# GpSimd's additions of gate weights placed behind a head's diagonal blocks and its substitution, and given out four copies late instead of two

## The chip, the cores and the metric

The kernel runs on one core of a Trainium2 chip. The metric is device microseconds of one execution. Times are medians of several runs; the profile is one further execution.

## The reference

One residual block: a gated delta rule and a Conformer convolution run side by side on `x` (512 tokens of 1024 channels), are merged by sigmoid gates, and are followed by a SwiGLU layer and a last RMSNorm.

```python
h = rmsnorm(x, norm1_w)
q, k, v, z, b_raw, a_raw, glu, gates = split(h @ w_in)           # 1024 -> 8208
q, k, v = silu(causal_depthwise_conv(q|k|v, dn_conv_w))          # 8 heads of 128
# per head, chunks of 64 tokens:
t_mat = I + strict_lower(beta * (k k^T) * decay)                 # 64 x 64, unit lower triangular
u, w  = triangular_solve(t_mat, [v * beta, k * beta * exp(gc)])
v_new = u - w S ;  o = (q exp(gc)) S + (q k^T * decay) v_new ;  S = S * el + k_dec^T v_new
out_a = (rmsnorm(o) * silu(z)) @ dn_w_o
out_b = silu(layernorm(conv31(ga * sigmoid(gb)))) @ cm_w_pw2 + cm_b_pw2
x = x + (gate_a * out_a + gate_b * out_b) @ w_out
f_gate, f_up = split(rmsnorm(x) @ ffn_w_gate_up)                 # 1024 -> 2 * 2816
x = x + (silu(f_gate) * f_up) @ ffn_w_down
return rmsnorm(x, norm_f_w)
```

## The kernel before

**Products.** Nearly all matrix products are `split3` (L124): operand and weight are each split into a high and a low part, and three matmuls are added in PSUM. `unit` (L108 to L115) prepares one weight block: SP loads `raw` (L108), ScalarE (ACT) makes the high part `whi` (L113), VectorE (DVE) the low part `wlo` (L115). Each has three buffers.

**Stages.** The first part (to about 430 us in the profile) is the head phase: for each of 8 heads, here numbered 0 to 7, come the projections, a 4-tap convolution, `front` (the triangular matrix `Un`), the substitution, and later `chain` (inverse and recurrence). Between them stand the projections of the convolution branch and of the gates. Then come `dn_w_o`, `cm_w_pw2`, `w_out`, the second norm, the SwiGLU layer in Strassen-like form, and the end.

**One head on GpSimd (POOL).** In `front`: the root `nk` (L474), `Un` times the decay (L485, 128x512), four copies of the diagonal 32x32 blocks into `cp` (L492), and `cc` put together from them (L493 to L495). SP stores `cc` to DRAM and loads it back spread out as `U` (L497, L500). Then POOL inverts the 16x16 diagonal blocks in `y` by 15 steps of a multiplication and an addition (L508, L510): this is the substitution, and `last[0]` is its latest instruction. L448 adds the mask to the decays of two later heads. L666 takes the root for the output norm of a head that has ended.

**One head's chain.** `chain` joins the 16x16 inverses to 32x32, 64x64 and 128x128 blocks: ACT scales `y` into `YY` (L563, L564), DVE transposes it (L565) and adds (L568: `m`, 128x32, both inputs in SBUF), and TensorE (PE) multiplies (L532, in `group`, six products in pairs). The results go through ACT (`Q`, L577 and L593) and copies (L573, L585, L589). Then come four steps of the recurrence (L630, L631, L636, L644, L645 on PE; `w` L638 and `R` L641 on ACT; `o` L656 on DVE). Head h's chain runs while head h+1's `front` is under way.

**The gate weights' sums.** The SwiGLU layer needs sums of quarters of its weight, `s1` to `s4`, 19 of each. Each of the 76 is made ahead of time in DRAM: SP copies one quarter (L196, 256 KB), and when that has landed GpSimd adds another to it by a DMA that accumulates (L200). `feed_one` gives both out, one per prepared unit: the copy goes at the end of the list `begun`, and L200 is given out for the copy that is two behind. An L200 waits on POOL until its copy has landed, and POOL executes in order. SP also loads halves of the down-projection weight (L170), which POOL adds (L176) and stores (L177).

**What sets the order.** A scheduler places each engine's instructions by priorities and its own estimate of times; `issue_after` makes an instruction stand behind another one. On the chip each engine takes its list in order.

Of the kernel before, what the change touches and what calls it, by code (L numbers as in the profile page):

```python
# [10 lines left out]
ALU = mybir.AluOpType  # L11
# [13 lines left out]
START = 78  # L25
ROUND = 40
WARM = 9
OTHERS = (12, 12, 12, 12, 8, 8, 8, 8)
EPS = 1e-6

# [2 lines left out]
def block_kernel(ctx, tc, a):  # L33
    nc = tc.nc
    V, S, G, PE = nc.vector, nc.scalar, nc.gpsimd, nc.tensor
# [28 lines left out]
    half = small.tile([P, 1], F32, name="half")  # L64
# [31 lines left out]

    loads, start_feed, ahead, gps_ = [], [False], [False], []

    last = [None]

    def unit(ap, pool=None, after=None):

# [23 lines left out]
    def col_tile(ps, ap, xh, xl):  # L126
        hi, lo = unit(ap)
        for k in range(KD):
# [25 lines left out]
          for n, r, c in (("A11", 0, 0), ("A12", 0, 1), ("A21", 1, 0), ("A22", 1, 1))}  # L154


    feed = [("s1", 0), ("s1", 1)] + [(n, p + d + i) for p in range(0, FF - F0, 2)
                                     for n, d in (("s3", 0), ("s2", 0), ("s1", 2), ("s4", 0)) for i in range(2)]
    feed = [(*w, *{"s1": ("A21", gu["A22"]), "s3": ("A11", gu["A21"]), "s2": ("A11", sums["s1"]),
                   "s4": ("A12", sums["s2"])}[w[0]]) for w in feed if w[1] < FF - F0]  # L160
    fed, begun = [], []
# [28 lines left out]
    def feed_one(n=1):  # L190

        for _ in range(n):
            if feed:
                w, p, m, other = feed.pop(0)
                with tc.issue_after(loads[-1].ins):
                    nc.sync.dma_start(sums[w][p], gu[m][p])  # L196
                begun.append((sums[w][p], other[p]))
        while len(begun) > (2 if feed else 0):
            with tc.issue_after(fed[-1].ins) if fed else nullcontext():
                fed.append(nc.gpsimd.dma_start(*begun.pop(0), accum_op=ALU.add, max_dma_last_dim=2048))  # L200

    units, norming = [0], [False]
# [13 lines left out]
    with tc.tile_pool(name="st", bufs=2) as st:  # L216
# [43 lines left out]
        wps = psg.tile([P, T], F32, name="g")  # L260
        for i in range(WARM):
            PE.matmul(wps, warm.broadcast_to([P, P]), warm.broadcast_to([P, T]), start=True, stop=True)
# [10 lines left out]
        for k in range(KD):  # L273
# [3 lines left out]
                                   op0=ALU.mult, op1=ALU.subtract)  # L277
# [7 lines left out]
        ss = st.tile([P, 2, NT], F32, name="rms_ss", bufs=1)  # L285
# [60 lines left out]
        for k in range(2, 4):  # L346
# [6 lines left out]
                        in1=ss[:, 1].rearrange("p (n a) -> p n a", a=1).broadcast_to([P, NT, 16]), op=ALU.mult)  # L353
# [6 lines left out]
                        in1=rowp[:, 1:2, :].broadcast_to([P, NT, H]), op=ALU.add)  # L360
# [9 lines left out]
        with tc.issue_after(ln_.ins):  # L370
            for g_ in gated:
# [8 lines left out]
                        op=ALU.mult)  # L380
# [13 lines left out]
    def even_odd(t):  # L394
        return t.rearrange("p (q e) c -> p e q c", e=2)
# [40 lines left out]
    def tok(src, pool, tag):  # L436
        ps = pool.tile([P, 4, P], F32, name=tag)
        for n in range(NT):
            PE.transpose(ps[:, n, :], src[:, n, :], ident)  # L439
        return ps  # L440
# [20 lines left out]
    def front(h, kT, DT):  # L461
        sq = junk[:, 0:P]

        ss = gp.tile([P, 8, NT], F32, name="ss", bufs=5)
        ps = tok(kT, psg, "g")
        for n in range(NT):
            S.activation(sq, ps[:, n, :], AF.Square, accum_out=ss[:, 0, n:n + 1])
        kd = gp.tile([P, 3, P], F32, name="kd", bufs=3)
        for n in range(3):
            S.activation(kd[:, n, :], ps[:, n, :], AF.Copy, scale=kdf[:, n, h:h + 1])  # L470
        kk, rk, nk, nb2, b2 = ss[:, 3], ss[:, 4], ss[:, 5], ss[:, 6], ss[:, 7]
        V.tensor_scalar(out=kk, in0=ss[:, 0], scalar1=EPS, scalar2=None, op0=ALU.add)
        V.reciprocal(out=rk, in_=kk)
        G.tensor_tensor(out=nk, in0=kk, in1=root4, op=ALU.pow)  # L474
        V.tensor_tensor(out=nb2, in0=rk, in1=nbeta[:, :, h], op=ALU.mult)
        V.tensor_tensor(out=b2, in0=rk, in1=beta[:, :, h], op=ALU.mult)

        ps = psg.tile([P, 4, P], F32, name="g")
        for n in range(NT):
            PE.matmul(ps[:, n, :], kT[:, n, :], kT[:, n, :], start=True, stop=True)  # L480
        Un = gp.tile([P, NT, P], F32, name="Un", bufs=3)
        for n in range(NT):
            S.activation(Un[:, n, :], ps[:, n, :], AF.Copy, scale=nb2[:, n:n + 1])
        yield
        G.tensor_tensor(out=Un, in0=Un, in1=DT, op=ALU.mult)  # L485

        cp = gp.tile([P, NT, 32], F32, name="cp", bufs=3)
        cc = gp.tile([P, NT, 16], F32, name="cc")
        ct = gp.tile([P, NT, 16], F32, name="ct")
        for b in range(4):  # L490
            b32 = slice(32 * b, 32 * b + 32)
            G.tensor_copy(out=cp[b32].rearrange("p (e q) c -> p e q c", e=2), in_=even_odd(Un)[b32, :, :, b32])  # L492
        G.tensor_scalar(out=cc, in0=cp[:, :, 0:16], scalar1=mh1, scalar2=None, op0=ALU.mult)  # L493
        G.tensor_scalar(out=ct, in0=cp[:, :, 16:32], scalar1=mh2, scalar2=None, op0=ALU.mult)
        G.tensor_tensor(out=cc, in0=cc, in1=ct, op=ALU.add)  # L495
        sc = dram.tile([8, 16, NT, 16], F32, name="sc")
        nc.sync.dma_start(sc.rearrange("b k n c -> (b k) n c"), cc)  # L497
        U = gp.tile([P, 16, NT, 16], F32, name="U", bufs=2)
        for b in range(8):
            nc.sync.dma_start(U[16 * b:16 * b + 16].rearrange("p k n c -> p (k n c)"),  # L500
                              sc[b].rearrange("k n c -> (k n c)").partition_broadcast(16))

        y = gp.tile([P, NT, 16], F32, name="y", bufs=3)
        S.copy(out=y, in_=idc.rearrange("p (a c) -> p a c", a=1).broadcast_to([P, NT, 16]))
        for k in range(15):
            w = 15 - k
            tm = gp.tile([P, NT, 16], F32, name="ytm")
            G.tensor_tensor(out=tm[:, :, 0:w], in0=U[:, k, :, k + 1:],  # L508
                            in1=y[:, :, k:k + 1].broadcast_to([P, NT, w]), op=ALU.mult)
            last[0] = G.tensor_tensor(out=y[:, :, k + 1:], in0=y[:, :, k + 1:], in1=tm[:, :, 0:w], op=ALU.add)  # L510
        return ss, kd, b2, Un, cp, y
# [300 lines left out]
    def head(h, done):  # L812

        pk, pq = (yield from proj2()) if h == 0 else (None, None)
        k_ = yield from conv4(8 + h, "kT", pk)
        close()
        q_ = yield from conv4(h, "qT", pq)
        close()
        v = conv4(16 + h, "vT")
        for _ in range(2):  # L820
            next(v)
            yield
        DT = dts.pop(0)
        opening = front(h, k_, DT)
        if h == 0:
            with behind():
                next(opening)
            v_ = yield from v
        if raised:
            decay()  # L830
        if h % 2 == 0 and h + 2 < H:
            masked(h + 2, h + 3)
        with behind(), tc.issue_after(last[0].ins) if h else nullcontext():
            if h:
                next(opening)
            try:
                next(opening)
            except StopIteration as made:
                ss, kd, b2, Un, cp, y = made.value
        if h:  # L840
            v_ = yield from v
        pz = yield from proj(24 + h)
        z_ = zall[:, h, :]
        S.activation(z_, pz, AF.Silu)


        def second():
            Vp, at = front2(k_, q_, v_, DT, ss)
            done.append((h, k_, q_, ss, kd, b2, Un, cp, Vp, at, y, z_))
            yield 0  # L850

        chains.append([count[0] + 5, second()])
        yield
# [6 lines left out]
    def take(n):  # L860
        for _ in range(n):
            if next(rest, 0) == 0:
                return
            yield
# [4 lines left out]
    for h in range(H):  # L869
        queue.append(head(h, done))  # L870
        queue.append(take(OTHERS[h]))
    queue.append(rest)
    nh = 0
    while step() or chains:
        ahead[0] = count[0] >= 72
        start_feed[0] = count[0] >= 335
        if nh < H and count[0] >= START - 9 + 32 * nh + sum(OTHERS[:nh]):
            chains.append([0, chain(*done[nh])])
            nh += 1
        for c in list(chains):  # L880
            if c[0] <= count[0] or not queue:
                with behind():
                    n = next(c[1], None)
# [103 lines left out]
    def rms_half(ss, hf, n, cs, sq, last, y1=y1):  # L987

        S.activation(sq, y1[:, n, cs], AF.Square, scale=1.0 / 32, accum_out=ss[:, hf, n:n + 1])
        t = ss[:, 2, n:n + 1]  # L990
        G.tensor_scalar(out=t, in0=ss[:, hf, n:n + 1], scalar1=t if hf else EPS, scalar2=None, op0=ALU.add)
        if last:
            G.tensor_tensor(out=ss[:, 3, n:n + 1], in0=t, in1=half, op=ALU.pow)

    ss2 = mp.tile([P, 4, NT], F32, name="ss2", bufs=1)
    xs2 = mp.tile([P, NT, D], F32, name="xs2", bufs=1)
# [438 lines left out]
```

## Time and profile before

| what | value |
|---|---|
| median of 3 runs | 934.75 us (934.72, 934.75, 937.58) |
| the profiled execution's own time | 939.53 us |
| its span, first to last instruction | 937.8 us |
| granted TensorE clock, mean | 0.996 |
| busy: PE, DVE, ACT, POOL | 920.3, 766.0, 567.6, 354.4 us |
| POOL idle ahead of L200, waiting for copies | 181.6 us in 45 waits |

The profiled execution takes 4.8 us more than the median run; 1.7 us of its own time lie outside the span. PE is shown busy for 98% of the span, but a matmul's shown duration overlaps the next one, so the distance between starts tells more than the busy share. Times in rows are microseconds from the span's start.

### The profile page before, as it was taken

What the parts mean: (1) busy time and instruction counts of PE and PEld (TensorE: products, weight loads), DVE (VectorE), ACT (ScalarE), POOL (GpSimd) and SP (SyncE); (2) the same over time, 40 slices, a digit from 0 to 9 for tenths busy, and PEclk for the clock granted to TensorE, in tenths of its full rate; (3) what the DMA queues carried; (4) which work ended last, traced back from release to release, by engine and by line L of the source; (5) the groups of instructions that cost most, each with busy time, mean ns of one, the idle gap of its engine ahead of it and who ended that gap; (6) DMA issues with size and microseconds to landing.
All of it is one profiled execution on the core that took longest, in us unless ns stands there. A gap on an engine that the chain in (4) does not pass through costs nothing.

```text
span 937.8 us, 15306 instructions
## 1 busy us (share of the span) xinstructions
PE 920.3 (98%) x5204; PEld 793.4 (85%) x5204; DVE 766.0 (82%) x1207; ACT 567.6 (61%) x1295; POOL 354.4 (38%) x572
## 2 busy tenths in 40 slices
PE   9999999999999999999999999999999999999997
PEld 6778788888888888888888888889999999988886
DVE  4889898989989889999587543786787888889896
ACT  6687877898778796633565323454554444456545
POOL 0145366362654338534064252211033234133042
PEclk9999999999999999999999999999999999999999
DMA  9335766565755646988999998688677767577654
GB/s 309 127 113 180 183 181 157 141 188 114 184 137 149 166 112 198 309 251 270 277 283 302 289 262 213 195 212 250 214 258 243 264 214 258 183 241 253 211 183 154
DMA packets 90286, 197.62 MB, mean 211 GB/s; under 512 B 11424, under 2 KB 20816, under 8 KB 89184
## 3 DMA queue, kind: packets, MB, share of 16 engines
q1 hardware_dynamic: 75168, 161.93, 51.0%
q0 software_dynamic: 13744, 32.05, 17.8%
q10 hardware_dynamic: 1296, 2.67, 0.7%
q8 instruction: 41, 0.67, 0.3%
q14 instruction: 37, 0.30, 0.1%
HBM read 176.40 MB, written 60.05 MB: 252 GB/s over the span
## 4 chain that ended last, share of the span: by engine, by line
PE 76%; ACT 8%; DVE 6%; DMA 3%; issue 2%; SPq 0%; POOL 0%; POOLq 0%; ACTq 0%; DVEq 0%
PE mm L124 47%; PE w L124 23%; DVE wlo L115 3%; PE b L532 2%; ACT whi L113 2%; DMA raw<-s 2%; PE st L645 1%; DMA raw<-in_wgu_dram 1%; PE g L439 1%; DMA DT<-mrow 1%; PE st L636 1%; DVE acc L426 1%; PE st L644 0%; PE g L480 0%; ACT s L550 0%
## 5 line engine op out<-in xcount | busy, mean ns | idle before, releaser
L113 ACT ACTIVATE whi<-raw 128x1024 fp32r<-128x1024 f32 (+1 forms) x205 | 207.9, 1016 | 213.5 <-PE mm L124 112.1
L115 DVE TENSOR_TENSOR wlo<-raw,whi 128x1024 fp32r<-128x1024 f32 (+1 forms) x205 | 256.9, 1254 | 72.8 <-ACT whi L113 71.5
L124 PE MATMUL mm<-hh,whi 128*128 128x512 f32 (+1 forms) x612 | 236.1, 387 | 0.6 <-ACT hh L340 0.3
L124 PE MATMUL mm<-hh,wlo 128*128 128x512 f32 (+1 forms) x612 | 230.9, 378 | 0.0
L124 PE MATMUL mm<-hl,whi 128*128 128x512 f32 (+1 forms) x612 | 230.2, 376 | 0.0
L700 DVE SCALAR_TENSOR_TENSOR cps<-c,c31w,cps 128x512 f32<-128x512 f32 x224 | 167.9, 750 | 3.6
L124 PEld LDWEIGHTS mm<-hh,wlo 128*128 128x128 f32 x612 | 115.9, 189 | 19.0
L124 PEld LDWEIGHTS mm<-hh,whi 128*128 128x128 f32 x612 | 116.1, 190 | 17.5 <-ACT hh L340 0.8
L124 PEld LDWEIGHTS mm<-hl,whi 128*128 128x128 f32 x612 | 116.2, 190 | 16.2
L200 POOL DMA_DIRECT2D s<-s x38 | 32.7, 860 | 103.7 <-DMA s<-in_wgu_dram 95.8
L124 PE MATMUL w<-hh,wlo 128*128 128x256 f32 x244 | 69.2, 284 | 2.0 <-DVE wlo L115 2.0
L124 PE MATMUL w<-hh,whi 128*128 128x256 f32 x244 | 69.2, 284 | 0.1
L124 PE MATMUL w<-hl,whi 128*128 128x256 f32 x244 | 69.1, 283 | 0.0
L200 POOL DMA_DIRECT2D s<-in_wgu_dram x38 | 32.9, 873 | 90.9 <-DMA s<-in_wgu_dram 85.7
L1070 POOL TENSOR_TENSOR fm<-fm 128x256 f32<-128x256 f32 x33 | 31.9, 967 | 75.5 <-DVE s L1070 51.6
L426 DVE SCALAR_TENSOR_TENSOR acc<-mm,c4w,acc 128x511 f32<-128x511 f32 (+2 forms) x72 | 53.1, 742 | 3.0 <-ACT acc L423 2.9
L508 POOL TENSOR_TENSOR ytm<-U,y 128x60 f32<-128x60 f32 (+14 forms) x120 | 35.2, 293 | 47.2 <-DMA U<-sc 39.0
L176 POOL TENSOR_TENSOR wst<-wst 128x512 f32<-128x512 f32 x16 | 26.4, 1653 | 68.6 <-DMA wst<-in_wdn_dram 37.4
L124 PE MATMUL mm<-yl,whi 128*128 128x512 f32 x128 | 49.8, 389 | 0.0
L124 PE MATMUL mm<-yh,wlo 128*128 128x512 f32 x128 | 49.8, 389 | 0.0
L124 PE MATMUL mm<-yh,whi 128*128 128x512 f32 x128 | 49.8, 389 | 0.0
L124 PEld LDWEIGHTS w<-hh,wlo 128*128 128x128 f32 x244 | 46.8, 192 | 2.6 <-DVE wlo L115 2.6
(346 smaller groups left out, 2149.7 us busy)
## 6 DMA issues: line engine op xcount, KB each, us to landing
raw<-in_win_dram SPq DMA_DIRECT2D x61, 512.0 KB, 4.6
s<-in_wgu_dram SPq DMA_DIRECT2D x76, 256.0 KB, 5.1
raw<-s SPq DMA_DIRECT2D x76, 256.0 KB, 4.1
raw<-in_wgu_dram SPq DMA_DIRECT2D x25, 512.0 KB, 4.3
raw<-wsum SPq DMA_DIRECT2D x44, 256.0 KB, 4.1
s<-in_wgu_dram POOLq DMA_DIRECT2D x38, 256.0 KB, 5.7
s<-s POOLq DMA_DIRECT2D x38, 256.0 KB, 5.6
raw<-in_wdn_dram SPq DMA_DIRECT2D x33, 256.0 KB, 3.5
```

The source lines that it names most:

```text
L113: marked(S.activation(hi, raw, AF.Copy), "unit")
L115: marked(V.tensor_tensor(out=lo, in0=raw, in1=hi.bitcast(F32), op=ALU.subtract), "unit")
L124: marked(PE.matmul(ps, l, r, start=first and i == 0, stop=last and i == 2))
L176: G.tensor_tensor(out=o, in0=x, in1=y, op=ALU.add)
L200: fed.append(nc.gpsimd.dma_start(*begun.pop(0), accum_op=ALU.add, max_dma_last_dim=2048))
L426: marked(V.scalar_tensor_tensor(out=acc[:, s:], in0=ps[:, :T - s], scalar=c4w[:, j, k:k + 1], in1=acc[:, s:], op0=ALU.mult, op1=ALU.add))
L439: PE.transpose(ps[:, n, :], src[:, n, :], ident)
L508: G.tensor_tensor(out=tm[:, :, 0:w], in0=U[:, k, :, k + 1:], in1=y[:, :, k:k + 1].broadcast_to([P, NT, w]), op=ALU.mult)
L532: PE.matmul(ps[:, q, 0:w], stationary[:, q, :], moving[:, q, :], start=True, stop=True)
L636: PE.matmul(ps[:, 1, :], Y[:, n % 2 * 2 + n // 2, :], R, start=True, stop=True)
L700: V.scalar_tensor_tensor(out=acc if k < 30 else cv[i], in0=c[:, k:k + T], scalar=c31w[:, i, k:k + 1], in1=acc if k > 1 else cv[i], op0=ALU ...
L1070: return eng.tensor_tensor(out=out, in0=in0, in1=in1, op=op)
```

## The change

Three things. `LAG = 4`: an L200 is given out for the copy four behind instead of two. A list `held` takes L495 (the last instruction of a head's diagonal blocks) and the second norm's L991 and L993; while no L200 has been given out yet, the first one must stand behind the latest of `held`, later ones behind the L200 before. And while the head phase lasts (`len(gps_) == 1`), two of every four L200 must also stand behind the latest substitution (`last`), the others behind the latest of `held`. In the new file every line after L28 has a number one higher.

```diff
+LAG = 4
...
-    last = [None]
+    last, held = [None], []
...
-        while len(begun) > (2 if feed else 0):
-            with tc.issue_after(fed[-1].ins) if fed else nullcontext():
+        while len(begun) > (LAG if feed else 0):
+            with tc.issue_after((fed or held)[-1].ins), tc.issue_after((last if len(fed) % 4 > 1 and len(gps_) == 1 else held)[-1].ins):
                 fed.append(nc.gpsimd.dma_start(*begun.pop(0), accum_op=ALU.add, max_dma_last_dim=2048))
...
-        G.tensor_tensor(out=cc, in0=cc, in1=ct, op=ALU.add)
+        held.append(G.tensor_tensor(out=cc, in0=cc, in1=ct, op=ALU.add))
...
-        G.tensor_scalar(out=t, in0=ss[:, hf, n:n + 1], scalar1=t if hf else EPS, scalar2=None, op0=ALU.add)
+        held.append(G.tensor_scalar(out=t, in0=ss[:, hf, n:n + 1], scalar1=t if hf else EPS, scalar2=None, op0=ALU.add))
         if last:
-            G.tensor_tensor(out=ss[:, 3, n:n + 1], in0=t, in1=half, op=ALU.pow)
+            held.append(G.tensor_tensor(out=ss[:, 3, n:n + 1], in0=t, in1=half, op=ALU.pow))
```

POOL at head 1's `front`, before (the tiles `s_125`, `s_126`, `s_127` and `s_128` are s1, s2, s3 and s4):

```order
L510 TENSOR_TENSOR y<-y,ytm 128x4
L200 DMA s_125<-in_wgu_dram 128x512 x2
L200 DMA s_127<-in_wgu_dram 128x512
L474 TENSOR_TENSOR ss<-ss,root_85 128x4
L200 DMA s_127<-in_wgu_dram 128x512
L200 DMA s_126<-s_125 128x512
L485 TENSOR_TENSOR Un<-Un,DT 128x512
L492 COPY cp<-Un 32x128 x4
L493 TENSOR_SCALAR cc<-cp,cst 128x64
L494 TENSOR_SCALAR ct<-cp,cst 128x64
L495 TENSOR_TENSOR cc<-cc,ct 128x64
L200 DMA s_126<-s_125 128x512
```

The same place now:

```order
L511 TENSOR_TENSOR y<-y,ytm 128x4
L475 TENSOR_TENSOR ss<-ss,root_85 128x4
L486 TENSOR_TENSOR Un<-Un,DT 128x512
L493 COPY cp<-Un 32x128 x4
L494 TENSOR_SCALAR cc<-cp,cst 128x64
L495 TENSOR_SCALAR ct<-cp,cst 128x64
L496 TENSOR_TENSOR cc<-cc,ct 128x64
L449 TENSOR_TENSOR DT<-DT,cst 128x512
L509 TENSOR_TENSOR ytm<-U,y 128x4x15
```

Six L200 have left this stretch, five of them from ahead of L485; the first two now stand behind head 2's L495.

POOL behind head 7's substitution, before (`U` is also the buffer of the halves of the down-projection weight):

```order
L510 TENSOR_TENSOR y<-y,ytm 128x4
L666 TENSOR_TENSOR ss<-ss,half_83 128x4
L176 TENSOR_TENSOR U<-U 128x256 x4
L177 DMA wsum<-U 512x1x256
L200 DMA s_127<-in_wgu_dram 128x512
L176 TENSOR_TENSOR U<-U 128x256 x4
L177 DMA wsum<-U 512x1x256
```

The same place now:

```order
L511 TENSOR_TENSOR y<-y,ytm 128x4
L201 DMA s_127<-in_wgu_dram 128x512 x2
L201 DMA s_126<-s_125 128x512
L667 TENSOR_TENSOR ss<-ss,half_83 128x4
L201 DMA s_126<-s_125 128x512
L201 DMA s_125<-in_wgu_dram 128x512 x2
L177 TENSOR_TENSOR U<-U 128x256
L201 DMA s_128<-s_126 128x512
L177 TENSOR_TENSOR U<-U 128x256 x6
L178 DMA wsum<-U 512x1x256
```

Seven L200 and three additions of the second half now stand ahead of the first half's store. On SP only one row moves: the load of the third half stands one store, one weight load and one copy later.

On the other engines the scheduler's order is the same until the last product of head 3's chain; later some rows change places. ACT at head 6, before (`Vp` belongs to head 7's `front2`):

```order
L557 COPY s_466<-Un 64x2x64
L563 ACTIVATE YY<-y,cst 128x4x16
L564 ACTIVATE YY<-y,cst 128x4x16
L518 ACTIVATE Vp<-g,ss 128x128 x2
L638 ACTIVATE w<-st,ss 128x128
L641 ACTIVATE R<-st,sm 128x128
L518 ACTIVATE Vp<-g,ss 128x128 x2
```

The same place now:

```order
L558 COPY s_466<-Un 64x2x64
L639 ACTIVATE w<-st,ss 128x128
L642 ACTIVATE R<-st,sm 128x128
L564 ACTIVATE YY<-y,cst 128x4x16
L519 ACTIVATE Vp<-g,ss 128x128 x4
L565 ACTIVATE YY<-y,cst 128x4x16
```

`w` and `R` of head 5's recurrence now stand ahead of `YY` and `Vp`.

## The prediction

> **What bounds the kernel now.** I read the page's first lines, then who waited for whom on PE and on POOL.
>
> ```profile
> span 937.8 us, 15306 instructions
> PE 920.3 (98%) x5204; PEld 793.4 (85%) x5204; DVE 766.0 (82%) x1207; ACT 567.6 (61%) x1295; POOL 354.4 (38%) x572
> ...
> PE w L124 <- DVE wlo L115: 2.0, 3, 1.2
> PE b L532 <- DVE m L568: 1.8, 1, 1.8
> ...
> POOL s L200 <- DMA s<-in_wgu_dram: 181.6, 45, 13.0
> ```
>
> PE bounds the kernel nearly everywhere: time can only come from its few waits, the longest of which is one of 1.8 us in L532. POOL loses 181.6 us in front of L200, but is busy for 38%; that loss counts only where somebody waits for what stands behind an L200. So I asked the timeline of each engine around L532's wait (ACT, then POOL, DVE, PE), and the summary of line L568.
>
> ```profile
> 97.46 1.12 ACT L483 ACTIVATE Un<-g,ss 128x128 f32<-128x128 f32 x4
> ...
> 98.75 0.86 POOL L200 DMA_DIRECT2D s<-in_wgu_dram  x1 [2.85 <-DMA s<-in_wgu_dram]
> 103.06 0.81 POOL L200 DMA_DIRECT2D s<-s  x1 [3.45 <-DMA s<-in_wgu_dram]
> 103.62 1.54 POOL L485 TENSOR_TENSOR Un<-Un,DT 128x512 f32<-128x512 f32 x1
> ...
> 103.41 1.80 DVE L568 TENSOR_TENSOR m<-XX,YY 128x32 f32<-128x32 f32 x1
> ...
> 103.14 0.39 PE L124 MATMUL mm<-hh,wlo 128*128 128x512 f32 x1
> 105.36 0.59 PE L532 MATMUL b<-m,s 128*128 128x16 f32 x4 [1.83 <-DVE m L568]
> ...
> L568 DVE TENSOR_TENSOR m<-XX,YY x8: 180/181/1804, 103.4 to 378.1; 128x32 f32<-128x32 f32 x8
> ```
>
> Head 1's L485 could start when ACT ended `Un` at 98.58, but two L200 waiting for their copies hold POOL until 103.06, and L485 comes at 103.62. There it meets head 0's `m`, on which PE waits. `m` takes 1.80 us where the median of its eight is 0.18, and ends (105.21) with L485 (105.16): the two engines exclude each other here. So the additions do no harm by taking time; they put L485 in the one place where it stops PE.
>
> The wait costs more than itself: the view by stretches shows the clock that was granted.
>
> ```profile
> 101.70:105.10 3.40, 1.83 (x10) 1.23 (x8) 2.96 (x4) 2.91 (x13) 2.04 (x2) 1.00 0.80 155
> 105.10:108.50 3.40, 3.14 (x15) 2.61 (x16) 2.96 (x10) 2.48 (x10) 2.39 (x8) 0.81 0.36 63
> 108.50:112.00 3.50, 3.50 (x16) 2.89 (x16) 3.39 (x5) 2.25 (x11) 0.00 (x0) 0.70 0.51 152
> ...
> 783.00:786.40 3.40, 2.14 (x16) 1.75 (x15) 3.29 (x5) 2.34 (x4) 3.40 (x3) 1.00 0.13 22
> ...
> 107.41 0.63 PE L124 MATMUL mm<-hl,whi 128*128 128x512 f32 x1
> 110.40 0.63 PE L532 MATMUL b<-m,s 128*128 128x32 f32 x4
> ...
> 427.61 27.24 PE mm L124 x120
> ```
>
> PE is busy for 1.83 of the 3.40 us around the wait (first number after the length), and then the clock (third number from the end) falls to 0.81 and 0.70; the row 783.00 with 2.14 busy stays at 1.00. From 107.41 to 110.40 seven products start 0.43 us apart; at full clock it is 27.24 / 120 = 0.227.
>
> **The change part by part.**
>
> *Head 1's L485 moves from 103.62 to about 98.9* (DVE's `wlo` holds it until 98.88), with L492 to L495 behind it until about 102.8; no L200 is left there. `m` then takes 0.18 and ends at 103.59. The first product follows `m` by 0.15, so at 103.74 instead of 105.36: 1.62 earlier. The rest is limited by ACT:
>
> ```profile
> 103.66 0.98 ACT L573 COPY s<-s 32x64 f32<-32x64 f32 x4
> 105.99 0.20 ACT L577 ACTIVATE Q<-b 128x32 f32<-128x32 f32 x1 [1.34 <-PE b L532]
> ...
> 109.70 0.24 ACT L589 COPY s<-YY 32x64 f32<-32x64 f32 x1
> 111.06 0.22 ACT L593 ACTIVATE Q<-b 128x64 f32<-128x64 f32 x1 [1.12 <-PE b L532]
> ```
>
> `Q` (L577) stands behind the four copies, which end at 104.64, so it starts at 104.65 instead of 105.99: 1.34. Without the low clock the third product gains 7 x (0.427 - 0.227) = 1.40 more, 2.74 in all, and L593 could start at 108.32. But ACT is busy with L589 until 109.94 - 1.34 = 108.60. So from L593 on the chain is 111.06 - 108.60 = 2.46 earlier. This is the first term: **-2.5**, of which 1.3 is the wait and 1.1 the clock. PE has nothing else to wait for until 430 us that would swallow it, and later it is fully used, so it reaches the end.
>
> *Other heads' L485 and substitution.* Here an earlier POOL brings nothing, since `y` is used late:
>
> ```profile
> 129.87 0.21 POOL L510 TENSOR_TENSOR y<-y,ytm 128x4 f32<-128x4 f32 x1
> 142.03 0.34 ACT L563 ACTIVATE YY<-y,cst 128x64 f32<-128x64 f32 x1
> ```
>
> 12 us lie between head 1's last step and its first use. Cost 0; the same slack covers L200 that now stand between L495 and L508. Two such collisions of L485 are known; the second one does not follow an L200 and stays:
>
> ```profile
> 220.61 1.16 DVE L662 TENSOR_SCALAR ss<-ss 128x4 f32<-128x4 f32 x1
> ...
> 220.45 1.29 POOL L485 TENSOR_TENSOR Un<-Un,DT 128x512 f32<-128x512 f32 x1 [1.59 <-ACT Un L483]
> 223.72 0.49 PE L630 MATMUL st<-S,kT 128*128 128x128 f32 x2 [0.69 <-DVE o L656]
> ```
>
> *The 76 L200* are as many and as long as before:
>
> ```profile
> L200 POOL DMA_DIRECT2D s<-in_wgu_dram x38: 802/835/1180, 90.2 to 643.3; - x38
> ...
> 241.78 1.22 DVE L115 TENSOR_TENSOR wlo<-raw,whi 128x1024 fp32r<-128x1024 f32 x1
> ...
> 241.72 0.89 POOL L200 DMA_DIRECT2D s<-s  x1 [0.19 <-issue]
> ```
>
> 0.84 us each, and beside one of them DVE's `wlo` takes its usual 1.22: an L200 itself does not stop DVE. Their copies will mostly have landed, so most of the 181.6 us of waiting goes; POOL has room for it, so 0. They end a few places later; the last sums are read by SwiGLU's last blocks, over 100 us after 643. Moving copies and additions apart leaves the bytes the same: 0, with a bound of +-0.3 from scatter.
>
> *ACT's new order at head 6.* `w` and `R` stand ahead of `YY` and `Vp`:
>
> ```profile
> 340.93 0.49 PE L644 MATMUL st<-w,kd 128*128 128x128 f32 x2 [0.61 <-ACT R L641]
> ...
> 339.26 0.35 ACT L563 ACTIVATE YY<-y,cst 128x64 f32<-128x64 f32 x1
> ...
> 339.76 0.61 ACT L518 ACTIVATE Vp<-g,ss 128x128 f32<-128x128 f32 x2
> 340.26 0.36 ACT L638 ACTIVATE w<-st,ss 128x128 f32<-128x128 f32 x1
> ```
>
> L638 moves from 340.26 to about 339.3, before L644 asks for it, and the wait of 0.61 goes: **-0.6**. In return `m` of head 6 comes behind a `wlo` of 1.2 us. Bounds: -0.6 and +0.6 (the same again, lost); I take -0.6, since the wait is in a row and the loss isn't.
>
> **Sum:** -2.5 - 0.6 = -3.1. The profiled execution's 939.53 would become 936.4; it stands 4.8 above the median. On the median of 934.75 the same terms give 931.7 (-0.33%), if a plain run contains the low clock too.
>
> **The rivals.**
>
> *A, the forecast:* 931.7, between 930.5 and 933.
>
> *B, the low clock does not count.* If the median run had the wait but not the low clock, or if the clock falls for another reason, only 1.3 + 0.6 go: 934.75 - 1.9 = 932.8. [...] Against: the clock falls right behind the only stretch with so little work. [...]
>
> *C, another collision in its place.* Head 1's mask addition L448 now follows L495 directly and may meet the next SBUF-only DVE instruction of head 0's chain; at the price of the old one, the gain is gone: 934.7. Against: its data come by a transfer behind the store of `cc`.
>
> *D, slower: SP is held by the third half.*
>
> ```profile
> 361.58 4.04 POOL L176 TENSOR_TENSOR U<-U 128x256 f32<-128x256 f32 x4
> 365.92 0.84 POOL L177 DMA_DIRECT2D wsum<-U  x1 [0.30 <-POOL U L176]
> ...
> 370.62 0.59 SPq L170 DMA_DIRECT2D U<-in_wdn_dram  x1
> ...
> SPq L170 <- POOL y L510: 10.2, 1, 10.2
> ```
>
> The first half's store L177 now stands behind seven L200 (7 x 0.84) and three more additions (3 x 1.0), so at 365.92 + 8.9 = 374.8, and the third load, which waited 4.7 for it, comes at about 379.5 instead of 370.62. SP holds all weight loads behind it. A hold of 10.2 us shows no wait on PE, so it decides from there; beyond it, each us costs one. Copies that are late for these L200 (the longest wait was 13.0) could hold SP for 17, some 7 us too long: 931.7 + 7 = 938.7. Against: the copies are issued far ahead, and the load itself stands later on SP.
>
> *E, more goes than I count:* the collision at 220.61 shifts apart as well (0.7), with some of the smaller waits: 930.5.
>
> **How the numbers follow.** About 0.3% (2.8 us, so below 931.95) is what a measurement of this kernel can tell from no change. A 0.55, of which 0.34 below that bound and 0.21 above; B 0.14; C 0.09; D 0.12; E 0.10. Faster: 0.34 + 0.10 = 0.44; same: 0.21 + 0.14 + 0.09 = 0.44; slower: 0.12. The range leaves D out: from E less 1.0 for what small waits it may take (929.5) to C plus 0.8 of scatter (935.5). It holds both signs; A's own range is 930.5 to 933.
>
> **What would show it.** Right: no L200 between about 90 and 140; L485 of head 1 near 98.9; all eight `m` below 0.6 us; PE's wait for L568 gone; no stretch below clock 1.00 near 105; L644's wait at head 6 gone; POOL's wait in front of L200 far below 181.6. Wrong: a new PE wait on a DVE instruction that ends together with a POOL instruction (C), PE waiting for `wlo` around 380 to 400 (D), or a span 3 us shorter with unchanged plain runs (B).

## The result, and the profile after

The changed kernel takes 942.94 us in the median (6 runs, 939.86 to 945.07), the kernel before 935.75 (6 runs): a ratio of 1.0074, 95% interval 1.0057 to 1.0092. It is slower by 7 us, and it had been forecast at 931.7. The profiled execution takes 943.04 us, 0.1 above its median; the one of before, 939.53, lies 3 to 3.5 us above the median of that kernel's plain runs (936.0 to 936.5 in the later comparisons). One execution of a later kernel (by turns before) ran at a granted clock of 0.752 and took 1123.69 us; the interval given for that kernel leaves it out.

The page after, first lines:

```profile
span 941.2 us, 15286 instructions
PE 921.3 (98%) x5204; PEld 793.1 (84%) x5204; DVE 767.0 (81%) x1207; ACT 568.4 (60%) x1295; POOL 359.2 (38%) x572
```

The waits after, on TensorE (PE) and on GpSimd (POOL); behind the colon: us in total, times, longest:

```profile
PE st L631 <- DVE o L657: 4.6, 2, 3.9
PE w L125 <- DVE wlo L116: 1.5, 4, 0.5
PE st L645 <- ACT R L642: 1.0, 2, 0.6
...
POOL s L201 <- DMA s<-in_wgu_dram: 66.0, 17, 13.0
...
POOL s L201 <- DMA s<-s: 22.5, 3, 8.2
```

The wait of 1.8 us for `m` is gone. GpSimd's waiting ahead of the additions falls from 181.6 to 66.0 behind copies, while behind other additions (`s<-s`) it rises from 6.6 to 22.5. One new wait of 3.9 us stands at the top.

Place one, head 1, came out as forecast. The summary of `m`, GpSimd's row and the stretches around it (first number behind the length: PE busy; third from the end: granted clock):

```profile
L569 DVE TENSOR_TENSOR m<-XX,YY x8: 172/180/183, 101.9 to 379.2; 128x32 f32<-128x32 f32 x8
```

```profile
97.14 1.35 POOL L486 TENSOR_TENSOR Un<-Un,DT 128x512 f32<-128x512 f32 x1 [2.78 <-ACT Un L484]
```

```profile
101.20:104.60 3.40, 3.08 (x17) 2.15 (x16) 2.78 (x8) 3.33 (x15) 0.44 (x2) 1.00 0.35 99
104.60:108.00 3.40, 3.36 (x20) 2.64 (x19) 3.27 (x7) 3.23 (x17) 0.79 (x1) 1.00 0.83 199
```

L486 starts at 97.14 instead of 103.62, all eight `m` take 0.18, PE is busy for 3.08 where it was 1.83, and the clock stays at 1.00.

Place two is new. GpSimd, VectorE (DVE) and TensorE around 370 us after:

```profile
369.65 0.81 POOL L201 DMA_DIRECT2D s<-s  x1 [7.88 <-DMA s<-s]
370.21 4.44 POOL L177 TENSOR_TENSOR U<-U 128x256 f32<-128x256 f32 x6
374.36 1.07 POOL L178 DMA_DIRECT2D wsum<-U  x1
...
370.18 5.03 DVE L701 SCALAR_TENSOR_TENSOR cps<-c,c31w,cv 128x512 f32<-128x512 f32 x1
375.13 2.15 DVE L116 TENSOR_TENSOR wlo<-raw,whi 128x1024 fp32r<-128x1024 f32 x1
378.19 0.28 DVE L657 TENSOR_TENSOR o<-st,R 128x128 f32<-128x128 f32 x1
...
374.23 0.40 PE L125 MATMUL mm<-hh,wlo 128*128 128x512 f32 x1
378.52 0.49 PE L631 MATMUL st<-S,kT 128*128 128x128 f32 x2 [3.90 <-DVE o L657]
```

The same place before (GpSimd did its additions in fours; the tap took 0.75, at a time when none was under way):

```profile
367.29 4.50 POOL L176 TENSOR_TENSOR U<-U 128x256 f32<-128x256 f32 x4
...
373.76 0.75 DVE L700 SCALAR_TENSOR_TENSOR cps<-c,c31w,cv 128x512 f32<-128x512 f32 x1
```

Six additions of down weights (L177) follow each other on GpSimd right behind the issue of a gate addition (L201). DVE's first conv tap (a tap is one of the 31 multiply-adds of the convolution), which reads two tiles of SBUF (`c` and `cv`), takes 5.03 us instead of 0.75; it ends 0.57 us after the six. `wlo` behind it meets the next addition, at 375.12 (2.15 instead of 1.23). `o` comes at 378.19, and PE, which had started its last product at 374.23, goes on at 378.52: 4.29 less the 0.23 that one product takes is 4.06 us lost. Then the clock falls:

```profile
372.80:376.20 3.40, 1.82 (x8) 1.13 (x6) 3.40 (x2) 0.24 (x2) 3.40 (x6) 1.00 0.45 106
376.20:379.60 3.40, 1.08 (x6) 1.02 (x7) 3.40 (x9) 1.05 (x6) 3.40 (x6) 0.96 0.90 197
379.60:383.00 3.40, 3.40 (x12) 2.80 (x11) 2.92 (x5) 2.15 (x5) 1.62 (x2) 0.53 1.04 251
```

A clock of 0.53 over 3.40 us is another 1.6 (3.40 x 0.47). In all some 5.7 us are lost here, by this estimate; the medians lie 7.2 apart.

Why six? GpSimd's list after, with what each row waits for (`U_4492` and `U_4630` are the first two halves; `Pool` stands for GpSimd's own instructions, `DMAHW` and `DMASW` for transfers: the L201 here is the one at 369.65, which waited 7.88 us for one):

```
L177 TENSOR_TENSOR U_4492<-U_4492 128x256 [waits DMAHW3_49]
L201 DMA s4_128<-s2_126 128x512 [waits DMASW6_49,DMASW2_49]
L177 TENSOR_TENSOR U_4492<-U_4492 128x256 [waits Pool_49]
L177 TENSOR_TENSOR U_4630<-U_4630 128x256 [waits DMAHW7_49]
L177 TENSOR_TENSOR U_4492<-U_4492 128x256 [waits Pool_49]
L177 TENSOR_TENSOR U_4630<-U_4630 128x256 [waits Pool_49]
L177 TENSOR_TENSOR U_4492<-U_4492 128x256 [waits Pool_49]
L177 TENSOR_TENSOR U_4630<-U_4630 128x256 [waits Pool_49]
L178 DMA wsum_129<-U_4492 512x1x256 [waits DMASW3_49,Pool_49]
L177 TENSOR_TENSOR U_4630<-U_4630 128x256 [waits Pool_49]
```

Seven L201 now stand behind head 7's substitution and push most of the first half's additions back until the second half has landed too. The scheduler then deals the two halves out by turns. Before, it gave four of one half, where each addition reads what the one ahead of it wrote.

### The profile page after: what moved, and what is told of

Its sections match the earlier page's. It is cut to its first block, busy times and chain, and to the rows that moved or that the text cites. A ratio compares the mean times of both kernels' runs of the same rounds, so it can differ in the third digit from the quotient of the medians.

```text
span 941.2 us, 15286 instructions
## 1 busy us (share of the span) xinstructions
PE 921.3 (98%) x5204; PEld 793.1 (84%) x5204; DVE 767.0 (81%) x1207; ACT 568.4 (60%) x1295; POOL 359.2 (38%) x572
## 4 chain that ended last, share of the span: by engine, by line
PE 67%; DVE 10%; ACT 9%; DMA 6%; issue 2%; SPq 0%; POOLq 0%; ACTq 0%; POOL 0%; DVEq 0%
PE mm L125 43%; PE w L125 18%; DVE wlo L116 5%; DMA raw<-s 3%; ACT whi L114 2%; PE b L533 2%; DMA sgd<-sg 1%; DVE cw L1071 1%; DVE cps L701 1%; DMA raw<-wsum 1%; PE g L440 1%; PE st L646 1%; PE g L481 1%; DVE acc L427 1%; PE st L637 1%
## 5 line engine op out<-in xcount | busy, mean ns | idle before, releaser
L116 DVE TENSOR_TENSOR wlo<-raw,whi 128x1024 fp32r<-128x1024 f32 (+1 forms) x205 | 254.2, 1241 | 74.3 <-ACT whi L114 70.6
L201 POOL DMA_DIRECT2D s<-s x38 | 39.9, 1161 | 55.9 <-DMA s<-in_wgu_dram 33.2
L177 POOL TENSOR_TENSOR wst<-wst 128x512 f32<-128x512 f32 x16 | 25.0, 1564 | 68.8 <-DMA wst<-in_wdn_dram 68.0
L201 POOL DMA_DIRECT2D s<-in_wgu_dram x38 | 37.8, 1173 | 33.0 <-DMA s<-in_wgu_dram 32.8
```

Source lines behind the costliest of these rows:

```text
L116: marked(V.tensor_tensor(out=lo, in0=raw, in1=hi.bitcast(F32), op=ALU.subtract), "unit")
L177: G.tensor_tensor(out=o, in0=x, in1=y, op=ALU.add)
```

## The experiments

Plain runs of the kernel before, shared by the comparisons, had medians of 936.0 to 936.5 us. Besides medians, I compare executions by the start of TensorE's n-th product, which is at the same place of the program in all of them (us, from the traces):

```
product   before  before   head 1  up to   after  after   only    in turn  in turn
          shown   again    alone   head 6  shown  again   head 7  first    again
 450      101.5   101.4     99.8   100.2   100.0   99.9    99.8    99.5     99.9
 600      134.2   131.6    130.0   130.5   130.2  130.1   130.0   129.7    130.2
1800      358.7   357.1    356.0   355.7   355.4  355.2   354.8   354.8    355.0
2100      416.7   415.2    414.0   413.7   419.6  418.0   418.7   414.3    419.9
```

**In turn.** The changed kernel, with the halves kept apart:

```diff
     def dsums_add(k, r, cs=slice(0, T)):
-        with tc.issue_after(last[0].ins):
+        with tc.issue_after(last[0].ins), tc.issue_after(summed[0].ins) if summed[0] else nullcontext():
             for o, x, y in ...:
-                G.tensor_tensor(out=o, in0=x, in1=y, op=ALU.add)
+                summed[0] = G.tensor_tensor(out=o, in0=x, in1=y, op=ALU.add)
```

> Changed kernel, with one thing more: a half's four additions of down weights are given out behind the last addition of the half before, so GpSimd does them half by half and no longer by turns from two halves. Theory of the train (the six additions by turns leave GpSimd no gap, DVE's first tap with two SBUF inputs waits 5.03 us through all of them, TensorE stalls 4.07 us behind it and then has a low clock): no DVE tap over 1.5 us near 370, no 4 us stall of TensorE at L631, and 943.0 - 4 to 7 = 936 to 939 against its plain runs, 931 to 936 if the 3.9 us that it is ahead at head 6 last to the end. Rival, the late loads (SyncE held some 11 us by the third half's load, copies given out four deep): SyncE is held as before and the time stays at 941 to 944. Rival, the new order of ScalarE's and VectorE's rows from head 6 on: also 941 to 944, since that order stays.

Median 940.62 us (938.14 to 947.58), 1.0053 of before [1.0033, 1.0073]; profiled execution 938.45. Only GpSimd's list differs from that of the changed kernel; the scheduler now puts five L201 between the additions of the two halves. The train and the 4 us stall are gone: from product 1800 to 2100 it takes 59.5 us, against 64.2 after and 58.0 before. What is left of DVE's waits there is smaller:

```profile
370.69 2.03 DVE L116 TENSOR_TENSOR wlo<-raw,whi 128x1024 fp32r<-128x1024 f32 x1
```

But the median falls by 2.3 only, to just above the range of the theory and below that of the rivals, so the train is not the whole loss, or something else takes its place.

**Lag two.** The changed kernel with `LAG = 2`.

> Changed kernel with LAG = 2 in place of 4: the additions of gate weights are queued behind the head's diagonal blocks and its substitution, but given out as early as before. The two halves' additions of down weights are still given out by turns, with a copy's issue ahead of them. Theory of the train: it stays and the time is 938 to 944, as far as a DVE instruction with two SBUF inputs meets it. Rival, the late loads: four copies are under way no longer, time back to 933 to 937. Rival, the order: 938 to 944.

938.59 us (935.29 to 941.88), 1.0024 [1.0009, 1.0040]. The halves still go by turns, and another instruction with two SBUF inputs stands in the train:

```profile
361.73 4.90 POOL L177 TENSOR_TENSOR U<-U 128x256 f32<-128x256 f32 x6
...
364.63 3.09 DVE L116 TENSOR_TENSOR wlo<-raw,whi 128x1024 fp32r<-128x1024 f32 x1
```

It waits 1.9 us (3.09 less its usual 1.23), until about the end of the six (366.5 against 366.63), but PE does not need that `wlo` yet (its only wait from 360 to 385 is one of 0.4). So the train costs by what stands in it. (This execution lost 4.9 us around product 3400 behind a late `whi`, which I did not follow up.)

**No substitution.** The changed kernel without the second condition:

```diff
-            with tc.issue_after((fed or held)[-1].ins), tc.issue_after((last if len(fed) % 4 > 1 and len(gps_) == 1 else held)[-1].ins):
+            with tc.issue_after((fed or held)[-1].ins), tc.issue_after(held[-1].ins):
```

> Changed kernel without the second condition: the additions of gate weights wait for a head's diagonal blocks (L496) alone, and not for its substitution; LAG stays 4. The halves' additions of down weights then come in groups of four of one half, as before the change. Theory of the train: no wait of DVE over 1.5 us from 355 to 380, head 1's part of the gain stays (L486 near 97 to 99 and its m under 0.6 us), 930 to 935. Rival, the late loads: four copies are still under way, 938 to 944. Rival, the order: between the two, 934 to 944.

937.16 us (934.27 to 942.62), 1.0010 [0.9991, 1.0029]: no different from before, and above the 930 to 935 of the theory. The additions go in fours again, and no DVE instruction from 355 to 380 takes 0.3 us more than it usually does. Four copies under way, kept here, cost nothing. But neither is there a gain, though head 1's `m` is in time.

**By turns before.** The kernel before, with the first two halves' additions forced by turns (A A, L200, B A B A B, store, B).

> Kernel before, with the additions of the first two halves of down weights forced by turns (A A, copy, B A B A B, store, B), all else as before. Theory of the train: the five by turns run from about 364 to 367.5 us without a gap, and a DVE instruction with two SBUF inputs that comes to stand in them waits to their end; before the change L115 stood at 361.99 and 367.52, so that the loss hangs on a few tenths: 0 to +5 us, 935.5 to 941, and whatever DVE instruction waits is one with two SBUF inputs. Rivals (late loads, order): no change, 935 to 936.5.

937.33 us (935.1 to 940.24 and the one of 1123.69), 1.0001 [0.9987, 1.0015]. The five by turns run from 364.57 to 368.37, and the one instruction with two SBUF inputs there, a `wlo` at 367.51, takes 1.96 instead of 1.23, near their end; at the same place in the execution shown of before, beside additions in fours, it took 2.05. No PE wait. This is at the low end of what was expected, and it tells little: the hit is a matter of tenths.

**Before again.** The kernel before, unchanged.

> Kernel before, unchanged, profiled once more. The profile shown of before took 939.53 us, its plain runs 936.4 us in the median, and the profile of the kernel with the additions by turns (940.24 us) has head 1's m late as well. Theory of the unlucky execution: m L568 at head 1 is late by 1.6 us only in some executions, those of 939 to 940 us; an execution of 934 to 937 us has it at 0.2 to 0.6 us, without the low clock behind it, so that the term of -2.5 us is no gain over the median. Rival: m is late in every execution of before, whatever the time, and the gain is real.

937.84 us. The summary of `m`:

```profile
L568 DVE TENSOR_TENSOR m<-XX,YY x8: 180/180/585, 103.3 to 376.6; 128x32 f32<-128x32 f32 x8
```

No late `m` at head 1: products 450 to 600 take 30.2 us, as in the changed kernel, where the execution shown of before took 32.7. The collision on which the first term rests is a matter of the single execution. Four traced executions have the old order at head 1. GpSimd starts L485 when the copies have landed, at 103.62 (before, shown), 101.96 (by turns before), 99.66 (here) and 102.88 us (before with stores by ScalarE, below); the first two have the late `m` (1.80 and 1.99 us), the other two have it at 0.18. How often plain runs have it is not known.

**Head 1 alone.** The kernel before, with the first six gate additions behind the diagonal blocks (`held` holds L495):

```diff
-            with tc.issue_after(fed[-1].ins) if fed else nullcontext():
+            with tc.issue_after((fed or held)[-1].ins), tc.issue_after(held[-1].ins) if len(fed) < 6 else nullcontext():
```

> Kernel before, with only the first six additions of gate weights queued behind the diagonal blocks of the latest head (L495), two under way as before; behind head 2 GpSimd's order is as before. It has the first term of the prediction and none of the rest. Theory of the unlucky execution: the profile shows m of head 1 under 0.6 us, and the plain runs are within 0.3% of before (935 to 938 us). Rival, the gain is real: 2.5 to 3.9 us below before, 932.5 to 934 us.

936.69 us (934.02 to 939.79), 1.0006 [0.9990, 1.0022]. Products 450 to 600 take 30.2 us and all `m` are under 0.73, so the first term is there in the trace; the median does not move. The interval allows a gain of 0.9 us at most, not 2.5.

**The trains alone.** Nothing of the block, only trains of additions and one multiply-add of DVE.

> A measurement by itself that leaves out all of the block (the output is the input): eight times GpSimd does a train of 128x256 additions, and VectorE one 128x512 multiply-add (the conv's form) that becomes ready at the train's start. In turn: two halves one after the other, each addition reads what the one ahead of it wrote; by turns: alternately from two halves. Order of the trials: in turn, by turns, in turn and by turns with an input in PSUM, by turns with four, by turns with six additions, in turn, by turns. Theory of the train: with two SBUF inputs VectorE's instruction takes 0.75 us plus at most one addition (under 1.6 us) where the additions go in turn, and 0.75 us plus the rest of the train by turns (about 3.5 us for four, 5 for six, 6.3 for eight); with a PSUM input 0.75 us in both. Rival, one instruction at a time (VectorE is served after the addition under way, whatever follows): under 1.6 us in all trials, and the 5.03 us had another cause.

The rival won. Eight by turns, with two SBUF inputs:

```profile
12.64 5.93 POOL L57 TENSOR_TENSOR h<-h 128x256 f32<-128x256 f32 x8
12.73 1.20 DVE L57 SCALAR_TENSOR_TENSOR cps<-c,go,cv 128x512 f32<-128x512 f32 x1 [0.31 <-POOL go L57]
```

1.19 to 1.20 in all trials with SBUF inputs, in turn or by turns: 0.45 us of waiting. With an input in PSUM 0.76. So additions by turns are not enough.

**The trains behind an issue.** What the trial lacked was the DMA issue right ahead of the six.

> The trains by themselves again (all of the block is left out), now with a DMA issue of GpSimd right ahead of the train, as L201 stands ahead of the six in the changed kernel, and with VectorE's multiply-add ready some 0.1 us into the train. Order of the trials: issue and eight additions in turn; issue and eight by turns; the same with an input of VectorE's instruction in PSUM; no issue and eight by turns; issue and four by turns; issue and six by turns; issue and four in turn; two issues and eight by turns; issue and eight by turns with VectorE's plain addition of two SBUF tiles. Theory of the train behind an issue (the issue makes each following addition start some 0.3 us before the one ahead of it ends, additions by turns keep that overlap, and VectorE gets no turn until it ends): about 6 us for eight, 4.7 for six, 3.3 for four by turns behind an issue; under 2 us for in turn, for no issue, and 0.75 for PSUM. Rival, one instruction at a time: under 2 us in all of them.

DVE's instruction in the nine trials, in the order of the text:

```profile
7.36 1.25 DVE L59 SCALAR_TENSOR_TENSOR cps<-c,go,cv 128x512 f32<-128x512 f32 x1
...
15.20 5.85 DVE L59 SCALAR_TENSOR_TENSOR cps<-c,go,cv 128x512 f32<-128x512 f32 x1
...
23.23 0.75 DVE L59 SCALAR_TENSOR_TENSOR cps<-c,go,acc 128x512 f32<-128x512 f32 x1
...
29.85 1.22 DVE L59 SCALAR_TENSOR_TENSOR cps<-c,go,cv 128x512 f32<-128x512 f32 x1
...
36.38 3.14 DVE L59 SCALAR_TENSOR_TENSOR cps<-c,go,cv 128x512 f32<-128x512 f32 x1
...
41.70 4.49 DVE L59 SCALAR_TENSOR_TENSOR cps<-c,go,cv 128x512 f32<-128x512 f32 x1
...
48.38 1.12 DVE L59 SCALAR_TENSOR_TENSOR cps<-c,go,cv 128x512 f32<-128x512 f32 x1
...
53.01 0.75 DVE L59 SCALAR_TENSOR_TENSOR cps<-c,go,cv 128x512 f32<-128x512 f32 x1
...
60.43 5.93 DVE L59 TENSOR_TENSOR sacc<-sacc,cv 128x512 f32<-128x512 f32 x1
```

GpSimd in the second trial:

```profile
14.44 0.56 POOL L59 DMA_DIRECT2D scr<-c  x1
15.01 5.47 POOL L59 TENSOR_TENSOR h<-h 128x256 f32<-128x256 f32 x8
```

Behind an issue and by turns, DVE waits for the whole train: 3.14, 4.49, 5.85 us for four, six, eight, that is 0.68 us for each addition. In turn behind an issue: 1.12 and 1.25. By turns without an issue: 1.22. Input in PSUM: 0.75. In these trials, each executed once, both conditions are needed, and the changed kernel made both. (The trial with two issues tells nothing: the instruction was ready at 53.01, before its train at 53.35.)

My picture of why was too definite: the additions here overlap by about 0.05 us (an estimate: trains of four, six and eight take 2.75, 4.12 and 5.47, so they start 0.68 apart and last some 0.73), not by 0.3 as in the changed kernel (0.98 long, 0.69 apart), and still hold DVE off. What the issue changes is open.

**After again.** The changed kernel, unchanged.

> Changed kernel, unchanged, profiled once more. Theory of the train: the six additions by turns and the tap or another DVE instruction with two SBUF inputs behind them are there again, since the order of the rows is fixed, with a wait of 2 to 5 us by where the tap comes to stand, and 940 to 945 us. Rival, chance: no DVE instruction waits over 1.5 us near 370 in this execution, and the time is 934 to 938 us.

940.03 us. Here the instruction ahead of the tap is caught:

```profile
369.39 4.08 DVE L706 TENSOR_TENSOR sacc<-sacc,cv 128x512 f32<-128x512 f32 x1
...
377.41 0.66 PE L631 MATMUL st<-S,kT 128*128 128x128 f32 x2 [2.97 <-DVE o L657]
```

Products 1800 to 2100 take 62.8 us. The hit recurs; its size depends on where DVE stands (3.0 us on PE here, 3.9 in the other).

**Up to head 6, and only head 7.** Two counterparts of the changed kernel:

```diff
 # up to head 6
-last if len(fed) % 4 > 1 and len(gps_) == 1 else held
+last if len(fed) % 4 > 1 and len(fed) < 26 else held
 # only head 7
-last if len(fed) % 4 > 1 and len(gps_) == 1 else held
+last if len(fed) % 4 > 1 and len(gps_) == 1 and len(fed) >= 26 else held
```

> Changed kernel, with the substitution's condition for the first 26 additions of gate weights alone: up to head 6 GpSimd's order is that of the changed kernel, behind head 7's diagonal blocks the copies no longer wait for the substitution, and the halves' additions come in fours of one half. Theory of the train: the loss sits behind head 7's substitution alone, so no DVE wait over 1.5 us from 355 to 380, and 935 to 938 us. Rival, the placing in heads 1 to 6 or four copies under way cost: 939 to 944 us.

> The counterpart: the substitution's condition from the 27th addition of gate weights on alone; up to head 6 they wait for the diagonal blocks only, and behind head 7 GpSimd's order is that of the changed kernel, with the additions by turns behind a copy's issue. Theory of the train: all of the loss is here, 940 to 944 us, with a DVE instruction with two SBUF inputs held 3 to 5 us near 370. Rival, the placing in heads 1 to 6 or the four copies cost: 935 to 938 us.

Up to head 6: 936.77 us (933.83 to 939.94), 1.0010 [0.9992, 1.0029]. Only head 7: 941.61 us (939.21 to 943.62), 1.0050 [1.0027, 1.0073]. "Up to head 6" has the changed kernel's order row for row on TensorE, VectorE and ScalarE, four copies under way, and GpSimd's list unchanged up to head 7's diagonal blocks; behind these GpSimd's list differs, and one row of SyncE. So neither the new order of the other engines' rows nor `LAG = 4` nor the placing in heads 1 to 6 makes the loss, as far as the interval tells: it is made behind head 7's substitution. Only head 7 shows the train and its victim:

```profile
368.09 0.81 POOL L201 DMA_DIRECT2D s<-s  x1 [6.34 <-DMA s<-s]
368.65 4.44 POOL L177 TENSOR_TENSOR U<-U 128x256 f32<-128x256 f32 x6
...
368.99 4.67 DVE L706 TENSOR_TENSOR sacc<-sacc,cv 128x512 f32<-128x512 f32 x1
...
377.57 0.49 PE L631 MATMUL st<-S,kT 128*128 128x128 f32 x2 [3.54 <-DVE o L657]
```

**In turn again.** Why is the kernel with the halves in turn still 4 us above before?

> The kernel with the additions half by half, profiled once more: its plain runs (938.1 to 947.6 us, median 940.6) lie above the time of its first profile (938.45 us), and 4 us above the kernel before. If what is left is the same mechanism (GpSimd's single additions right behind a copy's issue holding VectorE's instructions with two SBUF inputs), this execution shows one or more such waits of 1 us and more between 355 and 380, larger where the time is higher, and TensorE waiting behind them. Rival, the late loads: TensorE waits for a wlo whose raw load came late, between 380 and 400 or in the blocks behind 640.

944.20 us, and products 1800 to 2100 take 64.9. A `wlo` is held again (2.34 us at 370.49), but PE waits 0.4 at most behind it; the loss comes later. A load is late, as the rival had it, but no `wlo` waits for it: SyncE (SP) is held by the load of the next half (`SPq` rows are its transfers), and a store behind it is what somebody needs:

```profile
SPq L171 <- DMA wsum<-U: 23.8, 3, 13.7
```

```profile
379.92 0.59 SPq L171 DMA_DIRECT2D U<-in_wdn_dram  x1
...
387.02 0.59 SPq L171 DMA_DIRECT2D U<-in_wdn_dram  x1
387.71 0.57 SPq L714 DMA_DIRECT2D sgd<-sg  x1
...
389.77 0.69 ACT L713 ACTIVATE sg<-mm,vec 128x512 f32<-128x512 f32 x1 [4.16 <-DMA sgd<-sg]
...
392.18 0.80 PE L646 MATMUL st<-w,at 128*128 128x128 f32 x2 [3.30 <-ACT R L642]
```

The third half's load waits 13.7 us for the first half's store (before: 6.8), the fourth goes at 387.02. The store of a gate's sigmoid (L714) stands behind it on SP; ScalarE waits 4.16 for that buffer, `R` stands behind on ScalarE, and PE waits 3.3 and then has products 0.43 apart for a while. In the first profile of this kernel, where that store went just as late (387.81), the same wait of ScalarE was 0.4, and in the changed kernel 1.0, where the train had delayed ScalarE as well. One delay seems to cover the other; I did not test that.

**Stores by ScalarE.** The kernel with the halves in turn, and the kernel before, with that store issued by ScalarE (the scheduler moves some rows of ScalarE, VectorE and TensorE with it):

```diff
-        nc.sync.dma_start(sgd[i], sg)
+        nc.scalar.dma_start(sgd[i], sg)
```

> The kernel with the additions half by half, and the stores of the gates' sigmoid (L714) issued by ScalarE instead of SyncE; GpSimd's order is row for row that of the kernel with the additions half by half. Theory of the held store (what is left above the kernel before, 4 us in the median, is SyncE held by a half's load L171, with the sg store behind it, ScalarE waiting for the sg buffer at L713 and TensorE for R behind that): no wait of L713 for sgd over 0.5 us, and the median falls from 940.6 to 936 to 938.5, with the runs above 942 gone. Rival, the rest is single additions behind copies' issues: 939.5 to 942.

> Kernel before with the same move of the sg stores to ScalarE, as the control. Before the change SyncE is held by L170 for 6.8 us at the most behind a store of wsum, and no wait of L713 for sgd is seen. Theory of the held store: within 0.3% of before, 934.5 to 938. Rival, the move itself is a gain of its own: 931 to 934.

In turn: 938.34 us (934.49 to 943.90), 1.0024 [1.0006, 1.0042]: 2.3 below the same kernel with SyncE's stores. SP is still held for 14.2 us, but no L713 waits for `sgd`. Before: 936.46 us, 0.9999 [0.9987, 1.0011]: by itself the move does nothing. By the medians the held store was about half of what was left, but the intervals with and without it overlap, so its share is not settled; the expectation that runs above 942 would go failed (one took 943.9), and 1.8 us stay open.

No version came out clearly below the kernel before.

## Why the prediction was wrong

*Head 1's L485, -2.5.* Right in the trace, wrong for the median. From product 450 to 600 the changed kernel takes 30.2 us against 32.7 in the execution shown of before: 2.5, as summed. The step that failed is "On the median of 934.75 the same terms give 931.7 ... if a plain run contains the low clock too". A second execution of before has no late `m`, and the term alone (head 1 alone) gives 1.0006. The text itself noted that the profiled execution stood 4.8 above the median; the collision was part of that excess, and was then taken off a median that did not hold it, or not in full: L485 meets `m` only when the copies land at the wrong moment, in two of four traced executions.

*Moving other L485 and the substitution, 0.* Right: up to head 6 the whole placing measures 1.0010 [0.9992, 1.0029].

*The 76 L200, 0.* The step that failed worst. The page's groups show means of 1.16 and 1.17 us for an L201 (0.86 and 0.87 for an L200 before); that cost nothing clear of noise, since up to head 6 has 1.10 and 1.17 at a ratio of 1.0010. What cost is what they were put in front of. The text counted, under D, "seven L200 ... and three more additions" ahead of the first half's store, so it saw the halves run into each other, and priced only the delay of GpSimd's store (put at 374.8, it went at 374.36) and of the load behind it, not what the additions do to DVE. It also knew from head 1 that an instruction of GpSimd had held one of DVE there (`m` took 1.80 us beside L485 instead of 0.18), and from a `wlo` beside an L200 that "an L200 itself does not stop DVE" (1.22, its usual time). That row stands; but six additions by turns behind one held DVE's tap for 4.3 us (5.03 less 0.75), and PE for 4.1 plus 1.6 of low clock.

*ScalarE's new order at head 6, -0.6.* It hardly came: PE still waits 0.44 for `R` there after, against 0.61 before.

```profile
336.65 0.49 PE L645 MATMUL st<-w,kd 128*128 128x128 f32 x2 [0.44 <-ACT R L642]
```

*Rivals.* C had the right kind (a new collision of GpSimd and DVE that stops PE) in the wrong place and at half its size: "at the price of the old one", 3 us, where 5.7 went. D had the right place and a right mechanism: the third load was put at 379.5, and went at 377.99 after, and at 379.45 and 379.92 with the halves in turn; its price of 7 us met 5.4 (64.9 - 59.5, the two executions in turn). Only the waiting engine was another: not `wlo` behind weight loads, but ScalarE's sigmoid behind a store. No rival had both at once.

## What to carry over

A term read from one profiled execution may be taken off that execution's time; if the execution stands above the plain runs, ask first whether the term is part of the excess. When instructions of GpSimd move, write down the new neighbours on its list, what each of them waits for, and which VectorE instructions with two SBUF inputs fall beside them: additions by turns behind a DMA issue held such an instruction for the whole train here (it took 3.14 to 5.85 us in the trials, 5.03 in the changed kernel, and 0.75 with an input in PSUM). And a queue that is held (SyncE here, by a half's load, with 4.16 us of waiting on ScalarE and 3.3 on PE behind it) is priced by every transfer behind it, stores whose buffers somebody needs included.

## What was not expected of the hardware

VectorE's loss to GpSimd was not bounded by one instruction: behind an issue and by turns, its multiply-add with two SBUF inputs took 3.14, 4.49 and 5.85 us beside four, six and eight additions, 0.68 more for each. It took 1.22 without the issue ahead, 1.12 to 1.25 with additions that wait for each other, and 0.75 with an input in PSUM. In these trials a train takes 0.68 to 0.87 us for each of its additions (5.47 / 8 to 3.48 / 4). So without an issue or in turn VectorE lost 0.37 to 0.50 us over 0.75, less than one addition; behind an issue and by turns its instruction ended 0.57 us after the last of the eight (21.05 and 20.48).

The clock fell to 0.53 over 3.4 us after two stretches with PE busy for 1.82 and 1.08 of 3.40, and at head 1 before to 0.81 and 0.70 after a single one with 1.83.
